# A constant's tile of 64 columns in place of 32, at the foot of the lower half of the on-chip memory

## The chip, the core and the metric

The kernel runs on one core of a Trainium2 chip. The metric is the device time of one execution, in microseconds, as the median of several runs. The engines that matter are TensorE (PE, with its weight loads as PEld), VectorE (DVE), ScalarE (ACT), GpSimd (POOL) and SyncE (SP), which issues every DMA of this kernel.

## The reference, cut to what matters

One layer works on 1,024 latent tokens and 256 context tokens of width 1,024, in float32:

```
h  = rms_norm(x) * (1 + scale(c)) + shift(c)        # the context tokens likewise
p  = h @ w_in                                       # one projection, split in eleven parts
A  = bidirectional gated linear attention (4 heads, chunks of 64, decay per channel)
B  = differential attention (8 heads; softmax(q1 k1) - lam * softmax(q2 k2)) @ v
a  = rms_norm(A) * gla_norm * silu(gate_a)
b  = rms_norm(B) * diff_norm * (1 - lam_init) * silu(gate_b)
y  = sigmoid(m_a) * (a @ w_br_gla) + sigmoid(m_b) * (b @ w_br_diff)
out = x + g * (y @ w_out)
```

`gla_norm` has 256 values (two columns of 128) and `diff_norm` 128 (one column). Three columns hold these norm weights by channel.

## The kernel before, in words

**Products.** Nearly all time goes to matrix products of 128x128 weights with 512 columns of data. Each float32 operand is split in a high and a low part (`hi` by ScalarE, `lo` by VectorE), and three products replace one: high by high, high by low, low by high (`mm3`). In the profile every such product stands on line L349 (`mm`), transposes on L375 (`tr`). The names behind the arrow are, in this order, the moving operand and the weights: `mm<-w,g` streams 512 columns of a tile `w` against weights in a tile `g`. Buffer numbers are left out, so `g5` appears as `g`, `l5` as `l`, `x2` and `x4` as `x`, `e5` as `e`.

**Stages.** From 28 to 160 us come the first projections. From 160 to 500 us come projections done as block products with sums and differences of blocks, seven in place of eight (`pairs`). From 500 to 900 us come the remaining projections beside the gated linear attention. From 900 to 1480 us comes the differential attention (`s` scores, `b` transposes of the softmaxed scores and products with the values `vv`), with the gates and the first output products filled in between (`mb<-h,wt`). The last stage, to the end, is the second branch product and the output product (`mc`, `mz`, `mb`).

**Order.** A planner in the kernel (`Driver`) keeps a model of every engine's time while the program is built and writes the instructions of each engine in the order in which its model would run them. What is written is fixed: the chip follows semaphores. The planner's costs depend on sizes and kinds of operands, not on where a tile lies.

**Where tiles lie.** Each partition of the on-chip memory is filled from both ends. The pool of constants opens first, at the low end, then pools marked "left" are stacked above it and pools marked "right" below the high end, where a tile `edge` of 96 bytes is the first:

```
POOLS = dict(sbE="right", sb="left", sbK="left", sbA="left", sbB="left", sbC="left",
             sbA1="right", sbA2="right", sbW="right", sbG="right", sbF="right", sbD="right", ...
```

Left-hand tiles that the products read: `h` (`h0`, `h1`), `hk`, `w`, `p`, `pl`, `raw`, `at`, `vv`, `b1k`, `ya`, `yb`. Right-hand: `g` (`g5`), `l`, `x`, `wt`, `aq`, `xa`, `yc`, `wr`, `yd`, `e`, `ge`, `gp`, `gv`, `gkt`, `gso`. In the built program these left-hand tiles start at addresses that leave 256 when divided by 512 (for example `w` from 109,824 to 144,640, `h` from 17,664 on), and these right-hand tiles at addresses that leave 384 (`wt` from 208,768, `aq` from 192,384, `g` from 162,176). The operands of the 512-column products begin at multiples of 512 bytes into their tiles. The identity for transposes lies at 1,280, which leaves 256.

**The constants.** `gcol` (L466) is a tile in the constants' pool. Of its 32 columns three are used, by the scaling that follows each attention. It is opened in `consts_late`, after `ident` (the identity for transposes), `nhalf`, `ones`, `col`, `cs` and `gains`, and before the two tiny tiles `ls` and `nlam`.

Of the kernel before, what the change touches and what calls it, by code (L numbers as in the profile page):

```python
# [20 lines left out]
P = 128  # L21
# [211 lines left out]
class Hybrid:  # L233
# [222 lines left out]
    def consts_late(self):  # L456

        nc, a = self.nc, self.a

        def bc(ap, n):  # L460
            return ap.unsqueeze(0).to_broadcast([P, n])

        self.gains = g = self.c("gains", [P, 2, 2, 64])
        for i, nm in enumerate(("diff_q_norm", "diff_k_norm")):
            self.dma(g[:, i, 0], bc(a[nm][0], 64))
        self.gcol = self.c("gcol", [P, 32])  # L466
        self.dma(self.gcol[:, 0:2], a["gla_norm"][0].rearrange("(x p) -> p x", p=P))
        self.dma(self.gcol[:, 2:3], a["diff_norm"][0].rearrange("(x p) -> p x", p=P))
        yield from self.acq("p", 2)
        lp = self.t("p", [P, 4, 64])  # L470
        self.dma(lp, a["diff_lambda"][0].unsqueeze(0).to_broadcast([P, 4, 64]))
        yield self.d.when(lp)

        self.pool.tensor_scalar(g[:, 0, 0], g[:, 0, 0], 0.125, 0.0, ALU.mult, ALU.add)
        for i in range(2):
            gi, gr = (g[:, i, x].rearrange("p (x h e) -> p x h e", h=2, e=16) for x in range(2))
            for hh in range(2):
                self.pool.tensor_scalar(gr[:, :, hh], gi[:, :, 1 - hh], 1.0, 0.0, ALU.mult, ALU.add)
        self.pool.tensor_scalar(self.gcol[:, 0:2], self.gcol[:, 0:2], 0.5, 0.0, ALU.mult, ALU.add)
        self.pool.tensor_scalar(self.gcol[:, 2:3], self.gcol[:, 2:3], 1.0 - LAM_INIT, 0.5, ALU.mult, ALU.mult)  # L480
        lm = self.t("p", [P, 2, 64])
        self.dve.tensor_tensor(lm, lp[:, 0::2], lp[:, 1::2], ALU.mult)
        ls = self.c("ls", [P, 2])
        self.rel("p", self.dve.tensor_reduce(ls, lm, AX.X, ALU.add), 2)
        yield self.d.when(ls)
        yield self.act.activation(ls, ls, AF.Exp)
        self.nlam = self.c("nlam", [P, 1])
        self.dve.tensor_tensor(self.nlam, ls[:, 1:2], ls[:, 0:1], ALU.subtract)
        self.dve.tensor_scalar(self.nlam, self.nlam, LAM_INIT, None, ALU.subtract)
# [2321 lines left out]
```

## Time and profile before

| | before |
|---|---|
| median of 3 runs | 1627.62 us (1626.9 to 1630.98) |
| the profiled execution: its time / its span | 1627.54 us / 1625.8 us |
| PE busy | 1598.2 us, 98% of the span |
| PEld, DVE, ACT, POOL busy | 82%, 77%, 53%, 36% |
| granted TensorE clock | 0.998 |
| DMA | 346.72 MB, 213 GB/s on the mean |

The span runs from the first to the last instruction; the 1.7 us between it and the execution's time lie around it. A matmul's duration in the profile is longer than the step from one matmul to the next, because matmuls overlap: a product of 512 columns is given some 390 ns, and the next one starts some 230 ns later. A group's "busy" counts the overlap once, so busy time per instruction and mean duration differ.

### The profile page before, as it was taken

What the parts mean: (1) busy time and instruction counts of PE and PEld (TensorE: products, weight loads), DVE (VectorE), ACT (ScalarE), POOL (GpSimd) and SP (SyncE); (2) the same over time, 40 slices, a digit from 0 to 9 for tenths busy, and PEclk for the clock granted to TensorE, in tenths of its full rate; (3) what the DMA queues carried; (4) which work ended last, traced back from release to release, by engine and by line L of the source; (5) the groups of instructions that cost most, each with busy time, mean ns of one, the idle gap of its engine ahead of it and who ended that gap; (6) DMA issues with size and microseconds to landing.
All of it is one profiled execution on the core that took longest, in us unless ns stands there. A gap on an engine that the chain in (4) does not pass through costs nothing.

```text
span 1625.8 us, 24787 instructions
## 1 busy us (share of the span) xinstructions
PE 1598.2 (98%) x8333; PEld 1329.6 (82%) x8333; DVE 1249.4 (77%) x2209; ACT 857.8 (53%) x1771; POOL 583.2 (36%) x631
## 2 busy tenths in 40 slices
PE   8999999999999999999999999999999999999999
PEld 3788888888888888888888788888888888887887
DVE  4787957674756889879887588797877888878994
ACT  4776634443443463565644466566665565656331
POOL 1500000000001657445554146666755666660000
PEclk9999999999999999999999999999999999999999
DMA  8576898988878477776648544454587544356662
GB/s 314 185 256 242 319 339 286 321 321 298 314 268 271 145 223 235 224 241 194 208 135 231 185 117 131 129 159 125 152 262 219 161 143 127 107 182 234 228 205 95
DMA packets 275182, 346.72 MB, mean 213 GB/s; under 512 B 24136, under 2 KB 174320, under 8 KB 275056
## 3 DMA queue, kind: packets, MB, share of 16 engines
q1 hardware_dynamic: 275056, 345.14, 65.5%
q8 instruction: 66, 1.08, 0.3%
q14 instruction: 60, 0.49, 0.1%
HBM read 235.49 MB, written 109.58 MB: 212 GB/s over the span
## 4 chain that ended last, share of the span: by engine, by line
PE 85%; DVE 6%; ACT 3%; POOL 3%; issue 2%; DMA 1%; SPq 0%; ACTq 0%; POOLq 0%; DVEq 0%
PE mm L349 29%; PE mb L349 9%; PE s L349 7%; PE tp L349 7%; PE mc L349 7%; PE b L349 6%; PE gs L349 4%; PE b L375 4%; PE go L349 4%; PE gt L349 3%; DVE sm L201 2%; PE mz L349 2%; PE tp L375 2%; ACT e L201 1%; POOL at L201 1%
## 5 line engine op out<-in xcount | busy, mean ns | idle before, releaser
L349 PE MATMUL mm<-w,h 128*128 128x512 f32 x912 | 228.0, 398 | 0.0
L349 PE MATMUL mb<-h,wt 128*128 128x512 f32 x840 | 223.8, 402 | 0.8 <-DVE ft L201 0.5
L201 ACT ACTIVATE e<-s,sm 128x1280 f32<-128x1280 f32 x128 | 169.5, 1329 | 73.9 <-DVE sm L201 71.0
L201 DVE TENSOR_REDUCE sm<-s 128x1 f32<-128x1024 f32 (+1 forms) x192 | 193.5, 1036 | 18.0 <-PE s L349 14.2
L349 PEld LDWEIGHTS mm<-w,h 128*128 128x128 f32 x912 | 167.4, 189 | 32.5 <-DVE w L201 0.2
L201 POOL TENSOR_TENSOR at<-ac,at 128x512 fp32r<-128x512 f32 x128 | 188.9, 1476 | 10.7
L349 PEld LDWEIGHTS mb<-h,wt 128*128 128x128 f32 x840 | 151.7, 189 | 31.0 <-ACT ft L201 1.0
L349 PE MATMUL s<-hk,aq 128*128 128x512 f32 x744 | 170.5, 365 | 0.7 <-ACT e L201 0.4
L201 POOL TENSOR_SCALAR at<-ac 128x512 fp32r<-128x512 f32 x128 | 97.3, 760 | 195.1 <-ACT ac L201 191.4
L349 PE MATMUL mm<-h,w 128*128 128x512 f32 x672 | 163.7, 395 | 0.5 <-DVE h L201 0.5
L349 PEld LDWEIGHTS mm<-h,w 128*128 128x128 f32 x672 | 123.9, 189 | 26.1 <-DVE h L201 1.4
L349 PEld LDWEIGHTS s<-hk,aq 128*128 128x128 f32 x744 | 117.4, 189 | 18.5 <-ACT e L201 3.9
L349 PE MATMUL b<-at,vv 128*128 128x256 f32 x960 | 130.1, 287 | 1.1 <-ACT ac L201 0.8
L201 DVE TENSOR_TENSOR w<-raw,w 128x512 fp32r<-128x512 f32 x128 | 90.1, 725 | 52.5 <-ACT w L201 52.0
L201 POOL TENSOR_TENSOR sm<-sm,nhalf 128x2 f32<-128x2 f32 (+2 forms) x94 | 108.2, 1151 | 44.7 <-DVE sm L201 39.5
L349 PEld LDWEIGHTS b<-at,vv 128*128 128x128 f32 x960 | 119.6, 191 | 3.1 <-ACT ac L201 1.0
L201 DVE SCALAR_TENSOR_TENSOR e<-e,sm,e 128x1280 f32<-128x1280 f32 x64 | 120.4, 1881 | 0.7
L201 ACT ACTIVATE ac<-b 128x512 f32<-128x512 f32 x122 | 72.1, 598 | 81.7 <-PE b L375 81.3
L201 ACT ACTIVATE w<-raw 128x512 fp32r<-128x512 f32 x128 | 76.9, 626 | 65.0 <-PE go L349 16.6
L349 PE MATMUL mm<-w,g 128*128 128x512 f32 x432 | 108.6, 396 | 0.0
L349 PEld LDWEIGHTS mm<-w,g 128*128 128x128 f32 x432 | 81.4, 188 | 19.4 <-issue 0.5
L201 ACT ACTIVATE p<-mm 128x512 f32<-128x512 f32 (+1 forms) x104 | 59.9, 586 | 68.2 <-PE mm L349 53.7
(352 smaller groups left out, 3105.4 us busy)
## 6 DMA issues: line engine op xcount, KB each, us to landing
raw<-in_w_in SPq DMA_DIRECT2D x62, 512.0 KB, 5.0
g<-d_s SPq DMA_DIRECT2D x32, 640.0 KB, 6.5
gv<-d_v SPq DMA_DIRECT2D x80, 256.0 KB, 3.7
g<-d_s SPq DMA_DIRECT2D x32, 512.0 KB, 6.2
aq<-d_qT SPq DMA_DIRECT2D x124, 128.0 KB, 3.6
d_dv<-pl SPq DMA_DIRECT2D x40, 256.0 KB, 4.0
d_v<-pl SPq DMA_DIRECT2D x40, 256.0 KB, 2.6
d_kT<-pl SPq DMA_DIRECT2D x40, 256.0 KB, 2.5
```

What stands on the lines that cost most here:

```text
L201: self.ins = f(out, *args, **kw).ins
L349: self.ins = self.nc.tensor.matmul(out, lhsT, rhs, start=start, stop=stop, skip_group_check=more).ins
L375: self.nc.tensor.transpose(out, src, self.ident[:n, :n])
```

## The change

`gcol` is opened with 64 columns (256 bytes per partition) in place of 32 (128 bytes). The same three columns are written and read.

```
-        self.gcol = self.c("gcol", [P, 32])
+        self.gcol = self.c("gcol", [P, 64])
```

In the two built programs every engine has the same instructions in the same order with the same waits. What differs is addresses: `ls`, `nlam` and every tile of a left-hand pool, 2,098 in all, lie 128 bytes higher. The constants up to and with `gcol`, every right-hand tile (881 unmoved tiles together) and all 695 tiles of PSUM stay where they were. So the left-hand tiles named above start at addresses that leave 384 when divided by 512, as the right-hand ones do.

## The prediction

> **What bounds the kernel now.** I read the profile's page first: span, busy shares, and the chain of work that ended last.
>
> ```profile
> span 1625.8 us, 24787 instructions
> PE 1598.2 (98%) x8333; PEld 1329.6 (82%) x8333; DVE 1249.4 (77%) x2209; ACT 857.8 (53%) x1771; POOL 583.2 (36%) x631
> ...
> PE 85%; DVE 6%; ACT 3%; POOL 3%; issue 2%; DMA 1%; SPq 0%; ACTq 0%; POOLq 0%; DVEq 0%
> ```
>
> TensorE is busy 98% of the span and holds 85% of the chain. To see where it has slack I asked for busy time by stage (columns: length, then PE, PEld, DVE, ACT, POOL with counts, clock, DMA share, GB/s).
>
> ```profile
> 160.00:500.00 340.00, 340.00 (x1475) 277.07 (x1475) 230.05 (x357) 152.73 (x258) 4.05 (x3) 1.00 0.86 305
> 500.00:900.00 400.00, 395.76 (x2119) 336.60 (x2118) 323.33 (x628) 204.70 (x548) 207.13 (x264) 1.00 0.70 213
> 900.00:1480.00 580.00, 572.12 (x3431) 492.55 (x3430) 470.88 (x865) 344.74 (x704) 341.69 (x304) 1.00 0.52 154
> 1480.00:1626.00 146.00, 140.72 (x610) 113.90 (x608) 115.15 (x185) 54.14 (x99) 0.00 (x0) 1.00 0.59 200
> ```
>
> From 160 to 500 us TensorE has no idle time at all; elsewhere it lacks a few us per stage. The clock is full. So the time is the sum of the steps between matmuls, and a change that moves no instruction can act only if those steps depend on addresses. That is the question I put to the trace: do products of one shape take different times depending on where their operands lie? The groups of instructions from 160 to 500 us, shapes kept apart (after the bar: busy us, mean ns of one, idle before), answer it in one stage, at one clock, with no waits:
>
> ```profile
> L349 PE MATMUL mm<-w,g 128*128 128x512 f32 x396 | 99.6, 396 | 0.0
> L349 PE MATMUL tp<-w,h 128*128 128x512 f32 x240 | 58.0, 390 | 0.0
> L349 PE MATMUL gs<-w,g 128*128 128x512 f32 x132 | 37.9, 395 | 0.0
> L349 PE MATMUL mm<-w,h 128*128 128x512 f32 x144 | 34.6, 389 | 0.0
> L349 PE MATMUL gt<-w,h 128*128 128x512 f32 x142 | 34.3, 390 | 0.0
> L349 PE MATMUL tp<-w,g 128*128 128x512 f32 x120 | 29.6, 395 | 0.0
> L349 PE MATMUL gt<-w,g 128*128 128x512 f32 x96 | 23.6, 395 | 0.0
> L349 PE MATMUL go<-w,g 128*128 128x512 f32 x72 | 20.7, 395 | 0.0
> ```
>
> Every `w,h` product (both operands left-hand) takes 389 to 390 ns, every `w,g` product (weights right-hand) 395 to 396. The output bank does not matter: `tp` and `gt` occur with both. The last stage, as a timeline (start, us, operation, count), shows the same in unbroken streams:
>
> ```profile
> 1533.66 11.35 PE L349 MATMUL mc<-wt,h 128*128 128x512 f32 x48
> 1544.85 11.06 PE L349 MATMUL mc<-h,ya 128*128 128x512 f32 x48
> ...
> 1566.63 11.32 PE L349 MATMUL mc<-h,yc 128*128 128x512 f32 x48
> 1577.79 11.05 PE L349 MATMUL mc<-h,ya 128*128 128x512 f32 x48
> ```
>
> Forty-eight steps with one operand left and one right take 0.27 to 0.29 us more than with both left: 5.6 to 6.0 ns a step, as much as the durations differ, whether the right-hand tile is moving (`wt,h`) or holds the weights (`h,yc`). I call the two kinds "crossed" and "in step": crossed operands start 128 bytes apart modulo 256, in-step ones a multiple of 512 apart.
>
> Two readings are left: the relation of the two addresses matters, or each address by itself (a right-hand tile starts off a multiple of 256). Pairs with both operands right-hand decide, and there is one set: the products of `l` with `l`, scattered among left-hand products (duration as minimum, median, maximum):
>
> ```profile
> L349 PE MATMUL gs<-l,l x8: 392/393/500, 83.2 to 159.4; 128*128 128x512 f32 x8
> L349 PE MATMUL go<-l,l x8: 389/389/495, 83.6 to 159.7; 128*128 128x512 f32 x8
> ```
>
> `gs` comes first, straight after left-hand products, `go` second. `gs` is slow, but `go` has 389 ns, the in-step value, although both its operands are right-hand. So the relation counts, and a stream needs a product or so to settle.
>
> **The change part by part.** The larger tile costs no instruction and no byte of traffic. It moves all left-hand tiles by 128 bytes and no right-hand tile, so crossed pairs become in step and in-step pairs stay so.
>
> *160 to 500 us.* Crossed: 396 + 132 + 120 + 96 + 72 = 816 products. Each gains 395 − 389.5 = 5.5 ns: 4.5 us. TensorE is busy 340.00 of 340.00 us, so all of it is on the path.
>
> *900 to 1480 us.* The crossed groups, and what in-step products take in a stage that is as broken up by transposes and short products (500 to 900 us), as minimum, median, maximum; then the two large groups with shapes apart:
>
> ```profile
> L349 PE MATMUL mm<-w,h x768: 387/389/628, 511.7 to 877.8; 128*128 128x512 f32 x192
> ...
> L349 PE MATMUL mb<-h,wt x820: 387/393/500, 904.6 to 1479.9; 128*128 128x512 f32 x164
> L349 PE MATMUL mc<-h,wt x60: 390/393/482, 1442.7 to 1479.0; 128*128 128x512 f32 x60
> ...
> L349 PE MATMUL mc<-aq,hk x16: 390/393/404, 1465.0 to 1475.7; 128*128 128x512 f32 x16
> ```
>
> ```profile
> L349 PE MATMUL mb<-h,wt 128*128 128x512 f32 x820 | 219.0, 402 | 0.8 <-DVE ft L201 0.5 <-ACT ft L201 0.3
> L349 PE MATMUL s<-hk,aq 128*128 128x512 f32 x496 | 138.9, 400 | 0.5 <-ACT e L201 0.4
> L349 PE MATMUL s<-hk,aq 128*128 128x256 f32 x248 | 42.6, 294 | 0.2
> ```
>
> With the 496 of `s` and 32 `mc<-xa,hk` these are 820 + 496 + 60 + 32 + 16 = 1424 crossed products of 512 columns. Here I take the medians, 393 − 389 = 4 ns, since streams are short and settle anew: 5.7 us if all lies on the path. It does not. The chain within 900 to 1450 us, by line:
>
> ```profile
> by line: PE mb L349 24.6%; PE s L349 21.3%; PE b L349 15.7%; PE b L375 11.3%; DVE sm L201 5.9%; ACT e L201 4.0%; issue 3.8%; POOL at L201 3.8%; DVE e L201 2.4%; ACT ac L201 1.5%; DVE b1k L201 1.1%; POOL sm L201 0.8%; DVE at L201 0.8%; DVE h
> ```
>
> `mb` and `s` hold 45.9% of 550 us, 252 us, against 219.0 + 138.9 + 42.6 = 400 us of their busy time: 63%. Where the chain runs through VectorE, ScalarE or GpSimd, a faster product turns into a wait. That gives 3.6 us as the lower value and 5.7 as the upper; with TensorE busy 572 of 580 us I take 4.0.
>
> *1480 us to the end.* Crossed groups, first and last of nine with 274 products:
>
> ```profile
> L349 PE MATMUL mc<-h,yc 128*128 128x512 f32 x60 | 14.3, 395 | 0.0
> ...
> L349 PE MATMUL mb<-h,yc 128*128 128x512 f32 x12 | 2.9, 394 | 0.0
> ```
>
> At 5.5 ns they give 1.5 us, on the path.
>
> *What falls out of step.* The identity stays, so transposes of left-hand tiles (`p`, `b1k`) get the relation that `e` has now:
>
> ```profile
> L375 PE MATMUL b<-ident,e x610: 270/272/330, 920.4 to 1438.0; 128*128 128x128 f32 x153
> L375 PE MATMUL tp<-ident,p x145: 270/272/328, 5.1 to 891.6; 128*128 128x128 f32 x144, 40*128 40x40 f32 x1
> L375 PE MATMUL b<-ident,b1k x128: 270/272/330, 940.3 to 1476.3; 128*128 128x128 f32 x128
> ```
>
> Both relations have a median of 272 ns, so I price this at nothing; at most 1 ns for 273 transposes, 0.3 us. That is my allowance for the small things.
>
> *DMA.* Loads into and stores from left-hand tiles now start 128 bytes off a multiple of 256. Right-hand tiles already do (columns: count, KB each, median us to landing):
>
> ```profile
> x<-in_w_ada SPq DMA_DIRECT2D x8, 512.0 KB, 4.6
> l<-in_w_ada SPq DMA_DIRECT2D x4, 512.0 KB, 7.2
> raw<-in_w_ada SPq DMA_DIRECT2D x4, 512.0 KB, 5.9
> ```
>
> Equal loads into right-hand `x` and `l` lie on both sides of left-hand `raw`, 22% quicker and 22% slower; the side shows no order, so I take nothing. As a bound, 22% of the 1% of the chain that is DMA, 16 us, is 3.6 us either way. [...]
>
> Sum: 4.5 + 4.0 + 1.5 − 0.3 = 9.7 us. The profiled execution took 1627.54 us (span 1625.8), within 0.1 us of the median of 1627.62. So 1627.5 − 9.7 = **1617.8 us**. With 4 ns throughout, and 3 ns and 63% in the attention, the gain is 3.3 + 2.7 + 1.1 − 0.3 = 6.8 us, giving 1620.7; with 6 ns throughout and all on the path it is 4.9 + 8.5 + 1.6 = 15.0 us, giving 1612.5. The forecast's own range is 1612.5 to 1621; with DMA's bound on top it would end at 1624.
>
> **The rivals.** *Each address by itself.* If an operand must start at a multiple of 256, all left-hand operands lose that and today's in-step pairs become slow, while crossed ones stay slow. In-step products in the five largest groups number 912 `mm<-w,h`, 672 `mm<-h,w`, 240 `tp<-w,h`, 144 `gt<-w,h` and 144 `mc<-h,ya`:
>
> ```profile
> L349 PE MATMUL mm<-w,h 128*128 128x512 f32 x912 | 228.0, 398 | 0.0
> L349 PE MATMUL mm<-h,w 128*128 128x512 f32 x672 | 163.7, 395 | 0.5 <-DVE h L201 0.5
> ```
>
> 2112 times 5.5 ns is 11.6 us; with a fifth of the half that lies from 500 to 900 us hidden beside the linear attention, 10.4: 1638 us, slower. It decides as soon as a settled pair of two right-hand operands costs 395 ns. For it: `gs<-l,l` at 393. Against it: `go<-l,l` at 389.
>
> *Nothing happens.* The 6 ns could belong to the two ends of the memory rather than to the offset, since every crossed pair has one operand in each. Then the time stays 1627.5 us. For it: the trace has no crossed pair within one end. Against it, distance is no cause: by the built addresses `w,h` pairs lie 28 to 127 KB apart and take 389, `hk,aq` pairs 92 to 116 KB and take 400 on the mean. [...]
>
> **How the numbers follow.** Relation of addresses: 0.80, giving 1617.8. Nothing: 0.09. Each address by itself: 0.11. The range reaches from 1613 past the second case to 1628, and leaves out the slower case and the far end of the first. Under about 0.3%, 4.9 us, a measurement of this kernel cannot tell a difference; the forecast's own range, 6 us and more below, is beyond it, so the chances of faster, same and slower are these three.
>
> **What would show it.** Right: `w,g`, `h,wt`, `h,yc` and `wt,h` at 389 to 390 ns like `w,h`; streams of 48 in 11.05 us; transposes at 272; most of the gain before 500 us and in the attention; a little more idle time of TensorE between 900 and 1480 us. Wrong: `w,h` at 395 (each address counts), or `w,g` still at 395 (distance counts), or products at 389 with the time unchanged, which would mean that another engine or DMA ended the stages already.

## The result and the profile after

| | before | after |
|---|---|---|
| median of 6 runs each | 1627.53 us | 1620.01 us (1618.92 to 1623.69) |
| span of the profiled execution | 1625.8 us | 1618.2 us |
| PE busy | 1598.2 us | 1587.9 us |

The ratio is 0.9956, 95% interval 0.9942 to 0.997: 7.5 us faster. The page of after:

```profile
span 1618.2 us, 24787 instructions
PE 1587.9 (98%) x8333; PEld 1327.0 (82%) x8333; DVE 1248.6 (77%) x2209; ACT 857.3 (53%) x1771; POOL 583.7 (36%) x631
...
q1 hardware_dynamic: 275056, 345.14, 65.5%
...
PE 88%; DVE 4%; POOL 2%; DMA 2%; ACT 2%; issue 2%; SPq 0%; ACTq 0%; POOLq 0%; DVEq 0%
```

TensorE's busy time fell by 10.3 us; DVE, ACT and POOL moved by less than 1. The DMA queue's share (65.5%) is what it was before. The groups from 160 to 500 us, shapes kept apart, after:

```profile
L349 PE MATMUL mm<-w,g 128*128 128x512 f32 x411 | 101.0, 390 | 0.0
L349 PE MATMUL tp<-w,h 128*128 128x512 f32 x240 | 57.6, 389 | 0.0
L349 PE MATMUL gs<-w,g 128*128 128x512 f32 x135 | 38.0, 390 | 0.0
L349 PE MATMUL mm<-w,h 128*128 128x512 f32 x144 | 34.6, 389 | 0.0
```

`w,g` has come down from 395–396 to the 389–390 of `w,h`, which stayed. The unbroken streams of the last stage, as a timeline of after, show the same:

```profile
1526.97 11.04 PE L349 MATMUL mc<-wt,h 128*128 128x512 f32 x48
1537.86 11.04 PE L349 MATMUL mc<-h,ya 128*128 128x512 f32 x48
...
1559.62 11.04 PE L349 MATMUL mc<-h,yc 128*128 128x512 f32 x48
```

Forty-eight steps take 11.04 us in each of the three groups; crossed ones had taken 11.32 and 11.35. But between 900 and 1480 us (minimum, median, maximum, then the first and last start):

```profile
L349 PE MATMUL mb<-h,wt x828: 387/393/498, 900.5 to 1476.3; 128*128 128x512 f32 x166
L349 PE MATMUL s<-hk,aq x744: 274/390/501, 912.4 to 1425.4; 128*128 128x512 f32 x124, 128*128 128x256 f32 x62
L349 PE MATMUL mc<-h,wt x60: 387/389/477, 1437.6 to 1473.6; 128*128 128x512 f32 x60
```

`mb<-h,wt`, the largest group, still has a median of 393 ns. To place the gain I compare when the same instruction starts in the two traces, for the stage of block products by the group `tp<-w,h`, within 150 to 500 us, before and after:

```profile
L349 PE MATMUL tp<-w,h x240: 387/389/398, 165.1 to 497.6; 128*128 128x512 f32 x120
```

```profile
L349 PE MATMUL tp<-w,h x240: 389/389/389, 165.6 to 493.1; 128*128 128x512 f32 x120
```

| stretch | before | after | gain |
|---|---|---|---|
| to the first `tp<-w,h` | 165.1 | 165.6 | −0.5 |
| to the last `tp<-w,h` | 332.5 | 327.5 | 5.0 |
| to the first `mb<-h,wt` | 407.0 | 407.4 | −0.4 |
| to the first `mc<-h,wt` | 538.1 | 537.1 | 1.0 |
| to the end of the span | 183.1 | 180.6 | 2.5 |

This is one pair of traces. The kernels of the experiments below have the same instructions in these stretches, so their traces give the same stretches again. The block products, from the first to the last `tp<-w,h`, took 332.3 to 333.0 us in the four crossed kernels (this one among them) and 327.3 to 328.2 in the six in step. The attention, from the first `mb<-h,wt` to the first `mc<-h,wt`, took 538.1 to 538.4 us and 536.4 to 537.2. From the first `mc<-h,wt` to the end, where two of these kernels were changed and are left out, it took 182.2 to 183.1 us in three crossed traces and 180.6 to 181.8 in five in step.

So the block products gained the 4.5 us that was forecast, and a little more. The attention gained 1 to 2 us of 4.0. The last stage gained some 1.4 us between the means, about the forecast; the 2.5 of this pair is at the far end of its scatter.

### The profile page after: what moved, and what is told of

Read it like the earlier page. It is cut to its first block, busy times and chain, and to the rows that moved or that the text cites. A ratio compares the mean times of both kernels' runs of the same rounds, so it can differ in the third digit from the quotient of the medians.

```text
span 1618.2 us, 24787 instructions
## 1 busy us (share of the span) xinstructions
PE 1587.9 (98%) x8333; PEld 1327.0 (82%) x8333; DVE 1248.6 (77%) x2209; ACT 857.3 (53%) x1771; POOL 583.7 (36%) x631
## 3 DMA queue, kind: packets, MB, share of 16 engines
q1 hardware_dynamic: 275056, 345.14, 65.5%
## 4 chain that ended last, share of the span: by engine, by line
PE 88%; DVE 4%; POOL 2%; DMA 2%; ACT 2%; issue 2%; SPq 0%; ACTq 0%; POOLq 0%; DVEq 0%
PE mm L349 29%; PE mb L349 10%; PE s L349 8%; PE tp L349 7%; PE mc L349 7%; PE b L349 6%; PE b L375 4%; PE gs L349 4%; PE go L349 4%; PE gt L349 3%; PE mz L349 2%; PE tp L375 2%; POOL at L201 1%; DVE sm L201 1%; DMA w<-in_w_ada 1%
## 5 line engine op out<-in xcount | busy, mean ns | idle before, releaser
L375 PE MATMUL b<-ident,e 128*128 128x128 f32 x610 | 93.3, 273 | 2.3 <-ACT ac L201 0.8
```

The lines of the kernel that those rows point to most:

```text
L375: self.nc.tensor.transpose(out, src, self.ident[:n, :n])
```

## The experiments

Theory A: the step between two 512-column products depends on the relation of the two operands' addresses. Theory B: what counts is where the left-hand tiles lie.

**Moving the other side.** `gcol` keeps 32 columns.

```
-    EDGE = 96
+    EDGE = 224
```

> gcol keeps 32 columns; instead the edge tile at the high end grows from 96 to 224 bytes, so every right-hand tile lies 128 bytes lower and all tiles, the identity too, leave 256 modulo 512. Theory A (the relation of the two addresses counts): crossed pairs vanish as in the changed kernel, mm<-w,g at 389 to 390 ns, time 1620 us, 0.994 to 0.997 of before; if the transposes' relation helps streams to settle, up to 3 us less in the attention. Theory B (the new place of the left-hand tiles counts, whatever the others do): mm<-w,g stays at 395 to 396 ns and the time at 1627.5 us.

Measured: 1618.28 us, ratio 0.9939 (0.9922 to 0.9957). From 150 to 500 us:

```profile
L349 PE MATMUL mm<-w,g 128*128 128x512 f32 x405 | 99.5, 390 | 0.0
L349 PE MATMUL tp<-w,h 128*128 128x512 f32 x240 | 57.6, 389 | 0.0
```

With every left-hand tile back at its old place the gain is there. Theory B falls. Here the identity is in step too; whether that helps is left open, since the interval overlaps that of the change (0.9942 to 0.997).

**Moving both.**

```
-    EDGE = 96
+    EDGE = 224
-        self.gcol = self.c("gcol", [P, 32])
+        self.gcol = self.c("gcol", [P, 64])
```

> gcol has 64 columns and the edge tile 224 bytes: left-hand tiles 128 bytes higher, right-hand ones 128 bytes lower, so they are 128 bytes apart modulo 256 again. Theory A: mm<-w,g back at 395 to 396 ns, streams of 48 crossed products 11.32 us or more, time 1627.5 us, ratio 0.999 to 1.001. Theory B: as in the changed kernel, 389 ns and 1620 us.

Measured: 1627.6 us, ratio 1.0004 (0.9993 to 1.0015). From 150 to 500 us, and from 1480 us on:

```profile
L349 PE MATMUL mm<-w,g 128*128 128x512 f32 x396 | 99.6, 396 | 0.0
...
L349 PE MATMUL mc<-h,yc 128*128 128x512 f32 x60 | 14.3, 395 | 0.0
L349 PE MATMUL mc<-wt,h 128*128 128x512 f32 x48 | 11.4, 395 | 0.0
```

Each move alone gains about 0.5% (0.44 and 0.61), both together nothing: theory A. The larger constant by itself brings nothing.

**Sixty-four bytes apart.** `gcol` with 48 columns.

```
-        self.gcol = self.c("gcol", [P, 32])
+        self.gcol = self.c("gcol", [P, 48])
```

> gcol has 48 columns, so left- and right-hand tiles start 64 bytes apart modulo 256. Theory A with an all-or-nothing step (only multiples of 128 or 256 are clean): crossed products at 395 ns as before, 1627.5 us. Theory A with a cost that grows with the offset: about 392 ns and 1624 us. Theory B says nothing of 64 bytes; half the shift would give half the gain, 1624 us.

Measured: 1627.81 us, ratio 1.0 (0.9991 to 1.001). From 150 to 500 us, and from 1480 us on:

```profile
L349 PE MATMUL mm<-w,g 128*128 128x512 f32 x396 | 100.0, 397 | 0.0
...
L349 PE MATMUL mc<-wt,h 128*128 128x512 f32 x48 | 11.2, 392 | 0.0
```

Half the offset costs in time what the whole does. One group lies between, `mc<-wt,h` at 392; the large ones do not. It streams the right-hand tile and holds left-hand weights, the other way round from `mm<-w,g`, so at 64 bytes the direction of the offset may count. No run tested that.

**Two hundred and fifty-six bytes apart.** `gcol` with 128 columns.

```
-        self.gcol = self.c("gcol", [P, 32])
+        self.gcol = self.c("gcol", [P, 128])
```

> gcol has 128 columns: left-hand tiles 384 bytes higher, so that the two kinds start 256 bytes apart modulo 512. Theory A with a period of 256 bytes or less: 389 to 390 ns for mm<-w,g and 1620 us. Theory A with a period of 512 bytes: slower than 389 ns, 395 or another value, and 1627 us or so. This decides whether in step means a multiple of 256 or of 512.

Measured: 1616.79 us, ratio 0.9936 (0.9917 to 0.9954). From 150 to 500 us:

```profile
L349 PE MATMUL mm<-w,g 128*128 128x512 f32 x414 | 101.7, 390 | 0.0
```

A difference of 256 bytes is in step, with `w,g` at 390 ns: a period of 512 is ruled out. Since this kernel had the lowest median, it was timed again beside the changed one.

> The changed kernel once more, unchanged, beside the next one. Theory A: 0.9956 of before, 0.994 to 0.997.

> The kernel with gcol of 128 columns once more, to see whether it is faster than the changed kernel. Theory A: the two have the same relations everywhere, with the identity too, so they agree within 0.15%, and the 0.2% between their first medians was scatter. A rival, that a place 256 bytes further up is better still: 0.993 to 0.994 again, with 0.9956 for the changed kernel.

Measured: 1619.41 us, ratio 0.995 (0.9934 to 0.9967), for the change; 1620.13 us, ratio 0.9951 (0.9933 to 0.9969), for 128 columns. They agree, as theory A says of equal relations.

**Why the attention gained so little.** In the traces I took the steps from one start to the next between 900 and 1480 us. They are ordered by a 512-column product's place in its run, that is, in the unbroken row of such products since the last shorter one. The means are over steps under 250 ns; the second place is left out, because most of its steps are longer.

```
place in the run    3      4      5      6      7      9     10     13 and later
products          193    178    116    114     84     63     49    138 / 153
before, ns       231.1  232.5  231.5  232.3  234.5  232.6  232.5  232.1
after, ns        233.7  230.8  232.2  229.7  229.5  228.8  228.7  226.8
```

Up to the fifth place the two kernels do not differ one way. In step, a run reaches 227 ns on the mean only after some ten products, and most runs there are shorter (7.2 products on the mean, in both traces). That is theory S. To test it where nothing else is going on, the output product's runs were broken: every second step over `k`, its first product was split.

```
-                        e = self.mm3(pm, lh[:, cs], ll[:, cs], rh, rl, k == 0 and new, k == 3, not new)
+                        if k % 2:
+                            for z in (slice(0, 256), slice(256, 512)):
+                                self.mm(pm[:, z], lh[:, cs], rh[:, z], False, False, not new)
+                            self.mm(pm, lh[:, cs], rl, False, False, not new)
+                            e = self.mm(pm, ll[:, cs], rh, False, k == 3, not new)
+                        else:
+                            e = self.mm3(pm, lh[:, cs], ll[:, cs], rh, rl, k == 0 and new, k == 3, not new)
```

> The changed kernel (in step), but in the output product, the last 90 us, every second step over k has its first product of 512 columns split in two of 256 columns into the two halves of the same bank: the same work, while no run of 512-column products is longer than five. Theory S (a run of 512-column products needs some ten steps to settle after a break, whatever the relation): mc<-h,yc and mc<-h,ya rise from 389 to 393 ns and more on the mean. Rival theory N (the attention's products stay slow because of the neighbours there, the scores, transposes and other engines' work, not because of breaks): they stay at 389 to 390 ns.

> The same splitting in the kernel before (crossed). Theory S: mc<-h,yc and mc<-wt,h, now in runs of five, take about as long as in the broken kernel that is in step, within 1 to 2 ns, since neither settles: the advantage of 5.5 ns shrinks to a third or less, as it did in the attention. Theory N: the advantage stays whole, 395 against 389 ns.

Measured from 1535 us on, in step (`gcol` of 64 columns):

```profile
L349 PE MATMUL mc<-h,ya 128*128 128x512 f32 x120 | 32.2, 394 | 0.0
L349 PE MATMUL mc<-h,yc 128*128 128x512 f32 x50 | 13.6, 394 | 0.0
...
L349 PE MATMUL mc<-wt,h 128*128 128x512 f32 x17 | 4.0, 389 | 0.0
```

and crossed:

```profile
L349 PE MATMUL mc<-h,ya 128*128 128x512 f32 x120 | 32.2, 394 | 0.0
L349 PE MATMUL mc<-h,yc 128*128 128x512 f32 x50 | 13.6, 395 | 0.0
L349 PE MATMUL mc<-wt,h 128*128 128x512 f32 x48 | 11.4, 395 | 0.0
...
L349 PE MATMUL mz<-h,yc 128*128 128x512 f32 x20 | 5.5, 396 | 0.0
```

In runs of five, in-step products take 394 ns, crossed ones 395 to 396. (`mc<-h,ya` is in step in both kernels.) By the steps from start to start, the products with `yc` at the second to fifth place take 232.5 ns in step and 233.0 crossed. `mc<-wt,h`, just before, belongs to the branch product and was not broken, although the second expectation counts it among the broken ones; it keeps the whole advantage, 389 against 395. Breaking the run alone takes the advantage away, and the neighbours of the attention are not needed for it. Theory N falls as the whole account; whether neighbours add something is not shown. (One run each, 1622.61 and 1630.22 us; the time of the shorter products is in them.)

**Longer runs in the attention.** The fill-in products come up to twelve at a time, first in the kernel before (crossed), then with `gcol` of 64 columns.

```
                     step()
+                    while x[0] % 4 and not (kind and (rhs.ev[x[0], half].t is None or rhs.ev[x[0], half].t > d.now)):
+                        step()
                     yield AtPE(0)
```

> The kernel before (crossed), with the fill-in products of the attention written up to four steps over k at a time, twelve products in place of three, so that runs of 512-column products are longer there (in the order as built, 734 products stand at the sixth place of a run or later, against 489). It serves as the partner of the next kernel. Its own time may be better or worse than before by some us, since scores and transposes come later; no theory says which. Theory S: mb<-h,wt stays at a median of 392 to 394 ns, since crossed runs never settle.

> The same longer runs with gcol of 64 columns (in step). Theory S: more of the fill-in products settle, mb<-h,wt falls to a median of 389 to 391 ns, and the attention, from the first mb<-h,wt to the first mc<-wt,h of the output, gains 3 to 4 us on its crossed partner, where the changed kernel gained 2.6 on the kernel before. Rival theory N: 393 ns again and no more gain than 2.6 us there. Beside the changed kernel's 1620 us, 1617 us is the best to be hoped for, if the longer runs make nobody wait.

Measured: 1705.64 us crossed, ratio 1.0483 (1.0451 to 1.0515); 1693.79 us in step, ratio 1.0408 (1.0393 to 1.0424). Within 880 to 1750 us, crossed, and then the idle time in front of the scores and of the transposes of `b1k` (groups from 890 to 1560 us):

```profile
L349 PE MATMUL mb<-h,wt x888: 387/393/797, 904.6 to 1594.6; 128*128 128x512 f32 x178
L349 PE MATMUL mc<-wt,h x48: 387/394/399, 1611.3 to 1622.3; 128*128 128x512 f32 x48
...
L349 PE MATMUL s<-hk,aq 128*128 128x512 f32 x496 | 144.4, 412 | 8.2 <-ACT e L201 8.2
...
L375 PE MATMUL b<-ident,b1k 128*128 128x128 f32 x128 | 25.9, 286 | 18.1 <-ACT ac L201 12.2 <-DVE sm L201 2.8 <-ACT b1k L201 2.5
```

and in step:

```profile
L349 PE MATMUL mb<-h,wt x888: 387/390/629, 900.2 to 1583.0; 128*128 128x512 f32 x178
L349 PE MATMUL mc<-wt,h x48: 389/390/390, 1599.5 to 1610.2; 128*128 128x512 f32 x48
```

The median of `mb<-h,wt` falls to 390 ns once runs are longer. The stretch from the first `mb<-h,wt` to the first `mc<-wt,h` is 7.4 us shorter in step (699.3 for 706.7), where the change gained 2.6 (626.5 for 629.1). That is more than the 3 to 4 expected, but it is not a clean measure of settling: the granted clock differed between the two traces, 0.97 crossed against 1.00 in step from 950 to 1000 us and 0.93 against 0.97 from 1400 to 1500 us. So the median bears theory S out here, and the 7.4 us do not. As a kernel, both are 4 to 5% slower. TensorE is idle for longer before the scores (8.2 us for 0.5) and before the transposes of `b1k` (18.1 for 2.2), and the granted clock fell to 0.90 from 1500 to 1600 us (over the whole profiled execution it was 0.987 crossed and 0.988 in step, in the runs of the kernel before beside them 0.996 to 0.999); how much each costs was not taken apart. No version was found that beats the change clearly.

## Why the prediction was right or wrong

- **What bounds it.** Right: TensorE's steps are the time (PE was busy 1598.2 of 1625.8 us before and 1587.9 of 1618.2 after), and they depend on addresses (`w,g` took 395 to 396 ns before and 389 to 390 after). The forecast of 1617.8 lies 2.2 us below the measured 1620.01, and the range holds it. It is this close although one term of the sum is two to four times too large, since the term is small beside the whole time; of the forecast gain of 9.7 us, 7.5 came. No run shows the 0.3% below which the prediction saw no difference to be told; the interval measured here reaches 0.14% to either side of the ratio.
- **Relation, not place.** Right, and now shown from both sides (moving either end gains, both nothing). Operands 256 bytes apart modulo 512 were as fast as those 0 apart, 390 ns for `mm<-w,g` in both; the prediction had only multiples of 512 to go by. The two rivals fell with `w,h` at 389 and `w,g` at 390.
- **160 to 500 us.** Forecast 4.5 us, measured 5.0 (4.1 to 5.7 between any two of the traces).
- **The attention.** The failed step. "Here I take the medians, 393 − 389 = 4 ns, since streams are short and settle anew" gave 4.0 us; the traces gave 1 to 2 to the first `mc<-h,wt`, and `mb<-h,wt` stayed at 393. The products themselves hardly got faster: from 890 to 1560 us, as the rows below show, the busy time of `mb<-h,wt` fell by 1.6 us and that of the 512-column `s<-hk,aq` by 0.2, where 840 and 496 products at 4 ns would be 3.4 and 2.0. So the discount for the chain (63%) was not what was missing, and TensorE's idle time did not grow: PE was busy 572.29 of 580 us, against 572.12. The 389 was borrowed from a stage whose runs have eleven products on the mean; the attention's have seven, and there, after a shorter product, a run needs some ten steps (228.7 ns at the tenth place, 226.8 from the thirteenth on).
- **"A stream needs a product or so to settle."** This was read off `gs<-l,l` and `go<-l,l`, which in six of their eight pairs follow 512-column products without a break. It holds for such a change of tiles, and it is not the price of a break by a shorter product, which the attention has. After the change `gs<-l,l` has a median of 389 at once (rows below). The reading also overlooked the product ahead: before, the last `mm<-h,w` ahead of `gs<-l,l` took 396 ns in these six pairs, although its own operands are in step; after, 389.
- **The last stage.** Forecast 1.5 us, measured some 1.4 between the means, from the first `mc<-h,wt`, and 2.5 in the first pair of traces. The stretch includes 108 crossed products that my sum counted with the attention, 0.6 us at 5.5 ns. `mc<-h,h` fell from 394 to 390 ns in this pair, but it stands at 390 in the crossed kernels with both ends moved and with 64 bytes too, so that drop is scatter and not the change.
- **Left out of the sum.** From 500 to 900 us stand 48 more `w,g` products (36 `mm`, 12 `gs`), 0.3 us at 5.5 ns.
- **What falls out of step, and DMA.** Nothing, as priced: transposes of `p`, `b1k` and `e` keep a median of 272 ns, and the DMA queue's share is 65.5% as before. Of the loads into tiles that moved, the largest group, 62 of `raw<-in_w_in`, lands 5.1 us after issue in the median, against 5.0 before; loads of `in_w_ada` into `raw` land in 5.8 us against 5.9, and into the unmoved `x` and `l` in 4.6 and 7.3 against 4.6 and 7.2.

Rows of before and then of after, from 890 to 1560 us:

```profile
L349 PE MATMUL mb<-h,wt 128*128 128x512 f32 x840 | 223.8, 402 | 0.8 <-DVE ft L201 0.5 <-ACT ft L201 0.3
L349 PE MATMUL s<-hk,aq 128*128 128x512 f32 x496 | 138.9, 400 | 0.5 <-ACT e L201 0.4
```

```profile
L349 PE MATMUL mb<-h,wt 128*128 128x512 f32 x840 | 222.2, 400 | 0.8 <-DVE ft L201 0.5 <-ACT ft L201 0.2
L349 PE MATMUL s<-hk,aq 128*128 128x512 f32 x496 | 138.7, 400 | 0.6 <-ACT e L201 0.4
```

Rows of after for the products of `l` with `l` and for the transposes:

```profile
L349 PE MATMUL gs<-l,l x8: 388/389/400, 83.8 to 160.0; 128*128 128x512 f32 x8
L349 PE MATMUL go<-l,l x8: 389/389/486, 84.0 to 160.2; 128*128 128x512 f32 x8
```

```profile
L375 PE MATMUL b<-ident,e x610: 270/272/330, 916.1 to 1432.9; 128*128 128x128 f32 x153
L375 PE MATMUL tp<-ident,p x145: 270/272/329, 5.0 to 887.5; 128*128 128x128 f32 x144, 40*128 40x40 f32 x1
```

## What to carry to other kernels

Before costing a change that moves only addresses, group equal products by which tiles they read: one row pair (`w,g` 396, `w,h` 390) showed that addresses matter. If TensorE bounds a stage as it does here, try the moving operand and the weights a multiple of 256 bytes apart (0 and 256 modulo 512 gave 390 ns for `mm<-w,g`, 64 and 128 gave 396 to 397), and check it in the built program after every change of a tile's size. And take a settled value only for products in runs long enough to settle: a median from a stage with other run lengths is not the same price (in step, 389 ns where runs have eleven products on the mean, 393 for `mb<-h,wt` where they have seven). Before explaining a gain of a microsecond or two from one pair of traces, look how far the same stretch differs between traces of equal kernels.

## What the runs showed of the hardware

- In an unbroken run, a product of 512 float32 columns against 128x128 weights takes 227 ns from start to start when the two operands' addresses differ by 0 modulo 512 (`after`, `e1_right_down`) or by 256 (`e4_off256`). It takes 232 to 233 on the mean when they differ by 64 (`e3_off64`) or 128 (`before`, `e2_both_moved`), but for one group, `mc<-wt,h`, at 229 with 64. Why is not shown; the rival that only distance counts is out, since 128 bytes decide it (`mm<-w,g` at 396 ns in `before`, 390 in `after`).
- At 128 bytes, the weights of the next product count too. In `before`, 28 in-step products in the midst of in-step runs have a next product whose weights lie in the other half; they took 232.5 ns to its start, against 227.2 where the next weights are in step. In `after` the 28 took 226.9. This is read off the traces; no run separates a product's own weights from the next one's.
- After shorter products, in-step runs in the attention (`after`) need some ten steps to come down to 227 ns, from 230 to 234 on the mean at first; crossed runs (`before`) stay at 231 to 235. In runs of five, the products with `yc` take 394 ns in step (`e5_broken_in`) and 395 to 396 crossed (`e6_broken_crossed`), so the relation is worth about 1 ns there, where the unbroken `mc<-wt,h` shows 6 (389 and 395). The number of steps is not fixed: in the first projections of `after`, at five of the eight places, five steps of 228 to 236 ns follow the single 256-column product `gt<-l,l`, and then 227; at the same places in `before` the run went on at 226 to 227 ns at once. Why is not shown.
